# Issuing three chunks of block sums in the first FFN instead of beside the second mixer

## The chip, the cores and the metric

The kernel runs on one core of one Trainium2 chip. The time is the device time of one execution in microseconds, and the time of a kernel is the median of its runs. The profile is one further execution, recorded by the hardware profiler.

## What is computed

Two decoder layers over 512 tokens of 1024 features, in float32. Each layer adds a mixer (two kinds of attention side by side) and then a gated FFN to its input, with a normalisation before and after. The FFN matters here:

```python
def conv_ffn(h, w_up, conv_w, conv_b, w_down):
    u = causal_dwconv(h @ w_up, conv_w, conv_b)     # 1024 -> 2 x 2816, three taps along the tokens
    gate, up = jnp.split(u, 2, axis=-1)
    return (jax.nn.silu(gate) * up) @ w_down        # 2816 -> 1024
```

## The kernel before, in words

The order of the stages is `even` (first mixer), `ffn(0)`, `odd` (second mixer), `ffn(1)`. Every float32 operand of a large product is split into a high and a low part, and `mm3` (L343 to L347) makes three matmuls of each product: high by high, high by low, low by high.

**Weights.** The class `Weights` (L43) holds the list of all weight tiles in the order of their use. A tile of 128 by 1024 numbers is loaded from device memory by a DMA of the SyncE (SP) queue into one of three buffers `wraw` (`load`, L52 to L60). ScalarE (ACT) then makes the high part `wh` (L81) and VectorE (DVE) the low part `wl` (L82). There are five buffers for each part. A load can start when DVE has finished with the buffer's previous tile, and a split when TensorE (PE) has finished with a `wh`.

**The FFN's up stage.** `ffn` (L428) makes 22 pairs of output tiles, a gate and an up column block each, in the loop at L679 over `n`. Some of the pairs are made by a scheme of seven block products where the plain way has eight; that takes sums of blocks of the weights. `SEVEN` (L37) says which: in `ffn(0)` every second `n` from 4 to 18, in `ffn(1)` every `n` from 4 to 17.

- In `ffn(0)`, the sums of the weights' blocks are made on DVE from two raw tiles (`up_sums`, L175 to L202: L191, L192, L195 and L198 are the additions). Such a pair and the plain pair behind it need four loads together. `seven_sums` (L568) makes the products; two of its results, z2 (L587) and c22 (L591), are added on DVE and PE goes on adding to them.
- In `ffn(1)`, the sums come ready from device memory: `up_blocks` (L204) loads blocks of the tensors `ws` beside plain blocks (L57).

**The sums in device memory.** `make_sums` (L145 to L173) fills the `ws` tensors, for the 14 pairs of `ffn(1)`, in chunks of three pairs (`CHUNK`, five chunks). It uses only DMAs of the GpSimd (POOL) queue, from device memory to device memory, some of which add to what lies at the target. A chunk takes eight of them (`steps`, L164) in which each reads what the one before has written, at L161. The chunks of one call run four steps apart. Ahead of them, for each chunk, two DMAs of one number (L169) copy a `mark` into `ws`: the mark's only use is that the moves can't start before it is there. The call sets POOL's order by hand (`manual_schedule`, L166).

The first call (L1133) makes chunks 0 and 1 (`EARLY = 2`) during the first mixer. The second call (L1550) makes chunks 2, 3 and 4 in `odd`, behind its first projection. Its mark is a number that ACT copies into `lead` (L1549) from the last tile of that projection, `st`.

**What sets the order.** Where no order is written out by hand, the language's planner orders each engine's instructions at build time, by its own estimate of when each is ready. The up stage of `ffn(0)` and the first part of `odd` are ordered so, for PE, ACT and DVE; SP's queue always is. Each engine and each queue then runs its instructions in that fixed order, and one that waits holds up those behind it. Apart from DMA issues, POOL has only the small operations of the normalisations (L260 to L263).

Of the kernel before, what the change touches and what calls it, by code (L numbers as in the profile page):

```python
# [37 lines left out]
CHUNK = 3  # L38
PAIRS = len(SEVEN[1])
EARLY = 2  # L40
# [55 lines left out]
def trunk(tc, A, out):  # L96
    nc = tc.nc
    PE, ACT, DVE, POOL = nc.tensor, nc.scalar, nc.vector, nc.gpsimd

    with ExitStack() as top:  # L100
# [15 lines left out]
        def bank(tag, name, *shape):  # L116

            t = pp.tile([P, S], F32, tag=tag, name=name, bufs=BANKS[tag])
            if not shape:
                return t[:]  # L120
            n = math.prod(shape)
            names = "abc"[:len(shape)]
            return t[:, :n].rearrange(f"p ({' '.join(names)}) -> p {' '.join(names)}",
                                      **dict(zip(names, shape)))
# [4 lines left out]
        lead = cst.tile([P, 80], F32, tag="lead", name="lead")  # L129
# [15 lines left out]
        def make_sums(chunks, mark):  # L145

            wide = "(a q) c -> a (q c)"
            if not sums_of:
                sums_of[1] = [[dpool.tile([CHUNK * P, S], F32, tag=f"ws{j}{c}", name="ws")
                               for c in range(-(-PAIRS // CHUNK))] for j in range(4)]  # L150
            tiles = sums_of[1]

            def move(c, j, src, op=ALU.bypass):
                n = min(CHUNK, PAIRS - c * CHUNK) * P
                if src is None:
                    src = tiles[0][c][:n]
                elif src < 0:
                    src = tiles[1][c][:n]
                else:
                    src = A["ffn_up_q"][src, c * CHUNK * P:c * CHUNK * P + n]  # L160
                nc.gpsimd.dma_start(tiles[j][c][:n].rearrange(wide, q=4), src.rearrange(wide, q=4), accum_op=op,  # L161
                                    max_dma_last_dim=2048)

            steps = [(0, 3, ALU.bypass), (2, 2, ALU.bypass), (0, 2, ALU.add), (2, 0, ALU.add), (1, None, ALU.bypass),  # L164
                     (1, 0, ALU.add), (3, -1, ALU.bypass), (3, 1, ALU.add)]
            with tc.manual_schedule(engines={POOL.engine}):  # L166
                for c in chunks:
                    for j in (0, 2):
                        nc.gpsimd.dma_start(tiles[j][c][0:1, 0:1], mark)  # L169
                for n in range(len(steps) + 4 * len(chunks)):  # L170
                    for j, c in enumerate(chunks):
                        if 0 <= n - 4 * j < len(steps):
                            move(c, *steps[n - 4 * j])  # L173
# [169 lines left out]
        def mm3(o, lh, ll, rh, rl, first, last, more=False):  # L343

            PE.matmul(o, lh, rh, start=first, stop=False, skip_group_check=more)  # L345
            PE.matmul(o, lh, rl, start=False, stop=False, skip_group_check=more)  # L346
            PE.matmul(o, ll, rh, start=False, stop=last, skip_group_check=more)  # L347
# [80 lines left out]
        def ffn(layer, xnT, pending, final):  # L428
            with ExitStack() as es:
                fp = es.enter_context(tc.tile_pool(name=f"fp{layer}", bufs=1, reuse_waits="tile"))  # L430
                sp = es.enter_context(tc.tile_pool(name=f"fs{layer}", bufs=3, reuse_waits="tile"))
                cw = fp.tile([P, NF, 2, 4], F32, tag="cw", name="cw")
# [55 lines left out]
                def x_sums():  # L488

                    raw = [chp.tile([P, D], F32, tag="s", name="xsum") for _ in range(2)]  # L490
                    raw += [glob.tile([P, D], F32, tag=f"X{i}", name="xsum") for i in (3, 2)]
                    a, b, c, d = [r[:] for r in raw]

                    def whole_block(o, k0, t0):
                        h, l = x_block(k0, t0)
                        o = o.rearrange("p (a b) -> p a b", b=256)
                        DVE.tensor_tensor(o, h.bitcast(F32), l.bitcast(F32), ALU.add)

                    def sub(o, x, y):
                        DVE.tensor_tensor(o, x, y, ALU.subtract)  # L500

                    def minus(o, x, y):
                        DVE.scalar_tensor_tensor(o, x, -1.0, y, ALU.mult, ALU.subtract)

                    def parts(n, x):
                        h, l = sums[n]
                        return [lambda: ACT.copy(h[:], x), lambda: sub(l[:], x, h[:].bitcast(F32))]

                    return ([lambda: whole_block(a, 0, 0), lambda: whole_block(b, 0, 256), lambda: sub(a, a, b)]
                            + parts(0, a)  # L510
                            + [lambda: whole_block(c, 4, 256), lambda: sub(b, c, b)] + parts(2, b)
                            + [lambda: minus(c, c, a)] + parts(1, c)
                            + [lambda: whole_block(d, 4, 0), lambda: minus(d, d, c)] + parts(3, d))
# [96 lines left out]
                def begin_seven():  # L610

                    nonlocal begun
                    begun = [bank(t, "u") for t in "sa"]
                    c = begun[1][:, :256]
                    product(c, x_block(0, 0), True)
                    ACT.copy(begun[0][:, :256], c)
# [52 lines left out]
                def finish(left):  # L669

                    scale, conv, silu, rest = left
                    conv(0)
                    scale(1)
                    silu()
                    conv(1)
                    for step in rest:
                        step()

                for n, f in enumerate(PAIRED):  # L679
                    if n == 2:  # L680
                        for i in ORDER:
                            nc.sync.dma_start(spill[i * P:(i + 1) * P, :], X[i][:])
                    if n == (2 if final else 3):
                        for step in x_sums():
                            step()
                    if final and n == pairs[0]:
                        depth, W.depth = W.depth, 0
                        ready, stop = W.pos + 3, W.pos + (7 * PAIRS + 1) // 2 + 2
                        W.ahead(ready)
                        written = tc.manual_schedule(engines={PE.engine, DVE.engine, ACT.engine})  # L690
                        written.__enter__()
                        begin_seven()
                    if final and n in pairs:
                        left = seven(n, left)
                        if n == pairs[-1]:
                            for step in late:
                                step()
                            finish(left)
                            written.__exit__(None, None, None)
                            W.depth = depth  # L700
                        continue
                    u = u4[2 * n:2 * n + 2] if n < 2 else [bank(t, "u") for t in "sa"] if n in pairs else [None] * 2
                    y = sp.tile([P, 2, S], F32, tag="y", name="y")
                    if n in pairs:
                        seven_sums(u, y[:, 1, :256])
                    scale, conv, silu, rest = left = evict(n, y, u)
                    for z in range(2):
                        if u[z] is None:
                            u[z] = bank("as"[z], "u")
                            wh, wl = W.next()  # L710
                            for k in range(KD):
                                b = slice(k * P, (k + 1) * P)
                                mm3(u[z], wh[:, b], wl[:, b], xh[:, k], xl[:, k], k == 0, k == KD - 1)
                        if z == 0 or not final or n != pairs[0] - 1:
                            scale(z)
                        if not final or n != pairs[0] - 1:
                            conv(z)
                    if not final or n != pairs[0] - 1:
                        silu()
                        for step in rest:  # L720
                            step()
# [742 lines left out]
        def odd(xnT, pending, order):  # L1464
            xh, xl = xnT
            with ExitStack() as es:
# [59 lines left out]
                for i in ORDER:  # L1526
# [12 lines left out]
                    st = chp.tile([P, 512], F32, tag="s", name="vst")  # L1539
# [6 lines left out]
                nc.scalar.dma_start(tab12[:], A["dil_tab12"])  # L1546
                DVE.tensor_copy(tri[:], trif[:])

                ACT.copy(lead[0:1, 1:2], st[0:1, 0:1])  # L1549
                make_sums(range(EARLY, -(-PAIRS // CHUNK)), lead[0:1, 1:2])  # L1550


                for u in range(2):
                    proj_T(sq[u], 0.125, False, True)
# [319 lines left out]

        xnT = even()
        xnT = ffn(0, *xnT, False)
        xnT = odd(*xnT)
        ffn(1, *xnT, True)


# [101 lines left out]
```

## Time and profile before

| what | us |
|---|---|
| median of three runs | 1132.96 |
| lowest and highest run | 1132.69 and 1139.24 |
| span of the profiled execution | 1130.8 |
| time of that execution by the clock of the runs | not taken apart; the median lies 2.2 above its span |
| up stage of `ffn(0)` | about 236 to 446 |
| down stage of `ffn(0)` | about 446 to 580 |
| `odd` up to its output projection | about 580 to 762 |
| three chunks' moves on POOL, first to last issue | 613.5 to 747.4 |
| first load of a `ws` block for `ffn(1)` | 807.0 |

The span runs from the first to the last instruction of the profiled execution. A row of the view of groups or of the timeline gives an engine, a line, an operation, the tile written and the tiles read, the shapes, and times. A queue is written with a q behind its engine (SPq, POOLq). Idle time before an instruction stands in square brackets or behind a bar, with what ended it. In the view of stretches each engine has its busy time and its number of instructions.

### The profile page before, as it was taken

The page shows a single profiled execution, that of the slowest core. Times are in us where ns is not written, and L with a number is a line of the kernel's source. Part 1 is how long each engine was busy: PE and PEld are TensorE (multiplying, and loading weights), DVE is VectorE, ACT ScalarE, POOL GpSimd, SP SyncE. Part 2 cuts the span into 40 slices and gives each one's busy share as a digit, 9 for nine tenths or more (in the row PEclk, how much of TensorE's full clock was granted, in tenths as well). Part 3 has the DMA queues.
Part 4 walks back from the last instruction along what each step waited for, and adds up shares of the span by engine and source line. Part 5 has one row for each costly group of instructions (what it writes and reads, how often), then busy time and mean ns, then how long its engine had stood idle before and what let it go on. Part 6 is the DMA issues. An engine that isn't in the chain of part 4 may idle for free.

```text
span 1130.8 us, 17165 instructions
## 1 busy us (share of the span) xinstructions
PE 1118.5 (99%) x6432; PEld 951.1 (84%) x6432; DVE 898.1 (79%) x1526; ACT 624.9 (55%) x1060; POOL 96.0 (8%) x189
## 2 busy tenths in 40 slices
PE   9999999999999999999999999999999999999997
PEld 8876677898998998887888877888999999988886
DVE  6677476489998898898984476576889999989887
ACT  5565466446555555556653455575456666645662
POOL 2211012220000000000031111102000000000002
PEclk9999999999999999999999999999999999999999
DMA  8666731131422333354737878852335556524461
GB/s 296 197 180 137 215 109 57 57 134 57 130 94 79 128 94 121 99 168 151 226 128 227 206 186 202 217 122 85 110 112 182 179 182 196 177 89 148 144 205 75
DMA packets 61426, 166.82 MB, mean 148 GB/s; under 512 B 7841, under 2 KB 8993, under 8 KB 61217
## 3 DMA queue, kind: packets, MB, share of 16 engines
q1 hardware_dynamic: 47712, 132.65, 36.2%
q0 software_dynamic: 11712, 29.36, 11.8%
q10 hardware_dynamic: 1920, 3.74, 1.0%
q8 instruction: 50, 0.82, 0.3%
q14 instruction: 32, 0.25, 0.1%
HBM read 158.35 MB, written 35.68 MB: 172 GB/s over the span
## 4 chain that ended last, share of the span: by engine, by line
PE 88%; DVE 5%; DMA 3%; issue 2%; ACT 1%; POOL 0%; SPq 0%; POOLq 0%; DVEq 0%; ACTq 0%
PE u L345 12%; PE u L347 12%; PE u L346 12%; PE acc L345 4%; PE acc L346 4%; PE acc L347 4%; PE apt L345 3%; PE apt L346 3%; PE apt L347 2%; PE ao L345 2%; PE ao L347 2%; PE ao L346 2%; DVE wl L82 2%; PE sps L1170 2%; DMA wraw<-in_ffn_w_down 1%
## 5 line engine op out<-in xcount | busy, mean ns | idle before, releaser
L81 ACT CAST wh<-wraw 128x1024 fp32r<-128x1024 f32 (+1 forms) x235 | 240.7, 1033 | 158.0 <-PE u L346 51.6
L82 DVE TENSOR_TENSOR wl<-wraw,wh 128x1024 fp32r<-128x1024 f32 (+1 forms) x235 | 280.6, 1201 | 52.5 <-ACT wh L81 51.9
L345 PE MATMUL u<-xh,wh 128*128 128x256 f32 (+1 forms) x680 | 223.5, 329 | 0.0
L346 PE MATMUL u<-xl,wh 128*128 128x256 f32 (+1 forms) x680 | 223.1, 328 | 0.0
L347 PE MATMUL u<-xh,wl 128*128 128x256 f32 (+1 forms) x680 | 222.9, 328 | 0.0
L345 PEld LDWEIGHTS u<-xh,wh 128*128 128x128 f32 x680 | 129.2, 190 | 12.6 <-DVE u L587 1.3
L347 PEld LDWEIGHTS u<-xh,wl 128*128 128x128 f32 x680 | 129.1, 190 | 11.2 <-DVE wl L82 0.3
L346 PEld LDWEIGHTS u<-xl,wh 128*128 128x128 f32 x680 | 129.3, 190 | 11.0
L345 PE MATMUL acc<-wh,gh 128*128 128x512 f32 (+1 forms) x250 | 96.9, 388 | 0.8 <-DVE uu L758 0.8
L346 PE MATMUL acc<-wl,gh 128*128 128x512 f32 (+1 forms) x250 | 96.9, 388 | 0.0
L347 PE MATMUL acc<-wh,gl 128*128 128x512 f32 (+1 forms) x250 | 96.9, 387 | 0.0
L522 ACT ACTIVATE y<-u,cw 128x512 f32<-128x512 f32 x88 | 67.6, 777 | 36.9 <-PE u L347 33.4
L345 PE MATMUL u<-gh,wh 128*128 128x256 f32 x264 | 74.9, 284 | 0.1
L260 POOL TENSOR_TENSOR rv<-ms,epst 128x1 f32<-128x1 f32 x39 | 12.3, 314 | 736.3 <-ACT junk L312 351.2
L347 PE MATMUL u<-gh,wl 128*128 128x256 f32 x264 | 74.7, 283 | 0.0
L346 PE MATMUL u<-gl,wh 128*128 128x256 f32 x264 | 74.7, 283 | 0.0
L526 DVE SCALAR_TENSOR_TENSOR y<-u,cw,y 128x511 f32<-128x511 f32 x88 | 65.0, 743 | 3.5 <-ACT y L522 3.4
L528 DVE SCALAR_TENSOR_TENSOR y<-u,cw,y 128x510 f32<-128x510 f32 x88 | 65.3, 745 | 1.5
L345 PEld LDWEIGHTS acc<-wh,gh 128*128 128x128 f32 x250 | 46.9, 188 | 11.2 <-DVE uu L758 1.4
L347 PEld LDWEIGHTS acc<-wh,gl 128*128 128x128 f32 x250 | 47.0, 188 | 9.7
L346 PEld LDWEIGHTS acc<-wl,gh 128*128 128x128 f32 x250 | 47.0, 188 | 9.4
L345 PEld LDWEIGHTS u<-gh,wh 128*128 128x128 f32 x264 | 50.6, 192 | 1.3 <-ACT u L580 0.5
(371 smaller groups left out, 2420.8 us busy)
## 6 DMA issues: line engine op xcount, KB each, us to landing
wraw<-in_ffn_w_up SPq DMA_DIRECT2D x60, 512.0 KB, 3.7
wraw<-in_ffn_w_down SPq DMA_DIRECT2D x44, 512.0 KB, 3.7
ws<-in_ffn_up_q POOLq DMA_DIRECT2D x24, 768.0 KB, 7.6
wraw<-ws SPq DMA_DIRECT2D x56, 256.0 KB, 2.9
wraw<-in_ffn_up_q SPq DMA_DIRECT2D x42, 256.0 KB, 2.9
ws<-ws POOLq DMA_DIRECT2D x8, 768.0 KB, 6.4
wraw<-in_od_w_dqk SPq DMA_DIRECT2D x12, 512.0 KB, 4.4
wraw<-in_ffn_w_down SPq DMA_DIRECT2D x22, 256.0 KB, 2.8
```

The costliest lines, as they stand in the source:

```text
L81: self.nc.scalar.copy(h[:, :w], raw[:, :w])
L82: self.nc.vector.tensor_tensor(l[:, :w], raw[:, :w], h[:, :w].bitcast(F32), ALU.subtract)
L260: POOL.tensor_tensor(v[:, :n], ms, epst[:, :n], ALU.add)
L345: PE.matmul(o, lh, rh, start=first, stop=False, skip_group_check=more)
L346: PE.matmul(o, lh, rl, start=False, stop=False, skip_group_check=more)
L347: PE.matmul(o, ll, rh, start=False, stop=last, skip_group_check=more)
L522: ACT.activation(y[:, z], u[z], AF.Identity, bias=c[:, 3:4], scale=c[:, 2:3])
L526: DVE.scalar_tensor_tensor(y[:, z, 1:], u[z][:, :S - 1], c[:, 1:2], y[:, z, 1:], ALU.mult, ALU.add)
L528: DVE.scalar_tensor_tensor(y[:, z, 2:], u[z][:, :S - 2], c[:, 0:1], y[:, z, 2:], ALU.mult, ALU.add)
L1170: PE.matmul(s_ps[:, :w], mq[h][:, i * P:(i + 1) * P], mk[h][:, :w], start=True, stop=True)
```

## The change

The second call of `make_sums` moves from `odd` into `ffn`'s loop over `n`, at `n == 4` of `ffn(0)`, which is the first pair made of seven products. Its mark is now a number of `cw`, the tile of the convolution's coefficients, that is loaded once as `ffn(0)` begins (L433). The copy into `lead` in `odd` goes.

```diff
                     if n == (2 if final else 3):
                         for step in x_sums():
                             step()
+                    if n == 4 and not final:
+                        make_sums(range(EARLY, -(-PAIRS // CHUNK)), cw[0:1, 0, 0, 0:1])
                     if final and n == pairs[0]:
...
                 DVE.tensor_copy(tri[:], trif[:])
 
-                ACT.copy(lead[0:1, 1:2], st[0:1, 0:1])
-                make_sums(range(EARLY, -(-PAIRS // CHUNK)), lead[0:1, 1:2])
-
```

## The prediction

> **What bounds the kernel now.** I read the page's head first, then the chain of work that ended last.
>
> ```profile
> span 1130.8 us, 17165 instructions
> PE 1118.5 (99%) x6432; PEld 951.1 (84%) x6432; DVE 898.1 (79%) x1526; ACT 624.9 (55%) x1060; POOL 96.0 (8%) x189
> PE 88%; DVE 5%; DMA 3%; issue 2%; ACT 1%; POOL 0%; SPq 0%; POOLq 0%; DVEq 0%; ACTq 0%
> ```
>
> TensorE is busy for 1118.5 of 1130.8 us, so only 12.3 us of the span are without a matmul, and the chain lies on PE for 88%. Whatever moves can gain only where PE waits now, and lose only where it makes PE wait. So I compare the place that the three chunks leave with the place they go to, in the view of stretches (busy us of PE, PEld, DVE, ACT, POOL, each with its count; then PE's clock, DMA share, GB/s).
>
> ```profile
> 284.00:404.00 120.00, 119.93 (x758) 108.09 (x758) 109.89 (x159) 66.00 (x87) 0.00 (x0) 1.00 0.34 106
> 613.50:747.50 134.00, 133.31 (x768) 109.05 (x767) 80.12 (x196) 68.62 (x122) 17.93 (x24) 1.00 0.79 203
> 252.00:284.00 32.00, 32.00 (x184) 28.24 (x183) 30.67 (x40) 19.57 (x24) 0.00 (x0) 1.00 0.16 50
> ```
>
> The first row is the steady part of the first FFN's up stage: PE full, DVE at 92%, POOL empty, the DMA engines a third used. The second is the mixer while POOL issues the three chunks: PE idles 0.69 us, DVE is at 60%, the DMA engines are used to 0.79. The third is the start of the up stage, where DVE is at 96%. So the move takes DMA work out of a stretch where DVE has room and puts it into one where DVE has little.
>
> **Where the moved work would run.** POOL's timeline, and SP's row of the load that the new mark reads:
>
> ```profile
> 244.14 0.10 POOL L110 MEMSET spacer<- 128x1 f32 x1
> 568.56 0.73 POOL L260 TENSOR_TENSOR rv<-ms,epst 128x1 f32<-128x1 f32 x1 [324.32 <-ACT junk L312]
> 609.40 3.21 POOL L169 DMA_DIRECT2D ws<-lead  x6 [14.39 <-ACT lead L1549]
> 613.52 1.28 POOL L161 DMA_DIRECT2D ws<-in_ffn_up_q  x2 [0.90 <-DMA ws<-lead]
> 747.35 0.88 POOL L161 DMA_DIRECT2D ws<-in_ffn_up_q  x1 [3.53 <-DMA ws<-ws]
> 767.93 0.19 POOL L260 TENSOR_TENSOR rv<-ms,epst 128x1 f32<-128x1 f32 x1 [19.70 <-ACT junk L312]
> ...
> 243.95 0.38 SPq L433 DMA_DIRECT2D cw<-in_ffn_conv  x1
> cw<-in_ffn_conv SPq DMA_DIRECT2D x2, 88.0 KB, 3.8
> ```
>
> POOL does nothing between 244.14 and 568.56. The new mark needs only `cw`, issued at 243.95 and landed 3.8 us later, so about 247.8. The text puts the call at the fifth pair, but nothing on POOL waits for that pair, so I expect the six marks at about 248 and the first move about 4.1 us later (609.40 to 613.52 now), at 252. Should the planner put it at the fifth pair, at 284, the same sum holds with one pair later at either end.
>
> **The change part by part.**
>
> 1. Marks and moves on POOL: six issues of L169 in 3.21 us, then 24 of L161.
>
> ```profile
> L161 POOL DMA_DIRECT2D ws<-in_ffn_up_q x18: 575/916/1009, 613.5 to 747.4; - x18
> L161 POOL DMA_DIRECT2D ws<-ws x6: 591/616/927, 642.7 to 743.2; - x6
> L57 SPq DMA_DIRECT2D wraw<-ws x56: 319/323/1866, 807.0 to 959.1; - x56
> ```
>
> From first to last issue they take 133.9 us now, and PE sees nothing of POOL's own time. From 252 they would end at about 386. Behind them in POOL's queue stands the normalisation at 568.56, 182 us away: cost 0. Their readers, the loads of L57, begin at 807.0, which both places meet: 0. In the mixer POOL's next instruction is at 767.93, 20 us after the last move, so nothing waits for POOL there either: gain 0.
>
> 2. The copy at L1549 goes from ACT, and POOL's wait of 14.39 us with it. ACT is busy 68.62 of 134 us there: 0.
>
> 3. The mixer without the traffic. What does PE wait for there, and what do its loads cost?
>
> ```profile
> PEld run L1599 <- DVE z L1607: 1.6, 4, 0.6
> PEld z L1678 <- DVE st L1685: 0.7, 1, 0.7
> PEld z L1653 <- DVE wl L82: 0.7, 2, 0.4
> ACT wh L81 <- DMA wraw<-in_od_w_v: 0.7, 1, 0.7
> ACT wh L81 <- PE apt L346: 17.9, 7, 4.4
> ```
>
> These are us in total, times, longest. The first two are attention's own chain. Only 0.7 us wait for a weight, and ACT waits 17.9 us for PE to free a buffer, so the weights are ahead and a faster load buys little. Bounds: 0, and the three PE rows together, 3.0 us. The stretch's PE idle time, 0.69 us, is nearest; I take a gain of 0.5.
>
> 4. The first FFN's loads beside the traffic. The DMAs' bytes are the same in both places, so I take the traffic's share from the mixer (queue, packets, MB, share of 16 engines; first the up stage, then the mixer's two) and the landing times of `wraw` (min, median, max) in the same two stretches.
>
> ```profile
> q1 hardware_dynamic: 3456, 12.58, 33.1%
> DMA to landing us min/median/max: 3.3/3.7/4.9
> ...
> q0 software_dynamic: 6320, 16.25, 54.6%
> q1 hardware_dynamic: 4176, 10.86, 24.0%
> DMA to landing us min/median/max: 3.5/4.5/8.0
> ```
>
> 33.1% and 54.6% make 88%: the engines still suffice, and the moves should need little more than their 134 us. A load lands later by 4.5 - 3.7 = 0.8 us at the median and by 8.0 - 4.9 = 3.1 us at the worst. In the up stage loads come in close groups of three, like those that took 7 to 8 in the mixer, so I take the middle, 2.0 us. What covers it is the time from landing to use. One pair of tile pairs, in the timelines of SP, ACT, DVE and PE:
>
> ```profile
> 290.48 13.34 SPq L59 DMA_DIRECT2D wraw<-in_ffn_w_up  x2
> 305.77 2.12 SPq L185 DMA_DIRECT2D wraw<-in_ffn_w_up  x2
> 326.43 2.38 SPq L185 DMA_DIRECT2D wraw<-in_ffn_w_up  x2
> ...
> 308.70 1.05 ACT L81 CAST wh<-wraw 128x1024 fp32r<-128x1024 f32 x1 [0.99 <-PE u L346]
> 311.01 1.05 ACT L81 CAST wh<-wraw 128x1024 fp32r<-128x1024 f32 x1 [1.26 <-PE u L346]
> ...
> 312.45 1.22 DVE L82 TENSOR_TENSOR wl<-wraw,wh 128x1024 fp32r<-128x1024 f32 x1
> 314.73 0.68 DVE L191 TENSOR_TENSOR wraw<-wraw 128x512 f32<-128x512 f32 x1
> 315.33 0.42 DVE L591 TENSOR_TENSOR u<-u,y 128x256 f32<-128x256 f32 x1
> ...
> 316.11 0.28 PE L345 MATMUL u<-gh,wh 128*128 128x256 f32 x1
> ```
>
> The second load of the first row is issued at 290.48 + 13.34 - 0.33 = 303.49 (an issue takes 0.33), lands by the median at 307.2, and ACT uses it at 308.70, when PE frees a buffer: 1.5 us of cover. The next, at 305.77, lands at 309.5 and is used at 311.01: again 1.5. The third, at 307.56, lands at 311.3 for DVE's addition at 314.73: 3.4. With 2.0 us more the first two are 0.5 late, and the third is covered. ACT and DVE run in order, and DVE reaches L591 at 315.33 without a pause since 312.45. PE needs that sum at 316.11, 0.36 us after its end. So PE stalls between nothing (0.5 eaten by the 0.4 between the end of `wh` at 312.06 and DVE's start, and by the 0.36) and, with 3.1 late, about 0.8 to 2. I take 0.4 per pair of pairs, nearer the row than the worst. The pace is 20.6 us (326.43 - 305.77), so the moves from 252 to 386 lie beside the groups from 284 on, about six in all: 2.4 us, between 0 and 6 x 3.1 = 18.6.
>
> 5. The start, 252 to 284: DVE has 1.3 us to spare, and three loads lie there. I take 0.5, between 0 and 3.1.
>
> A rule bears on DVE beside POOL's issues. First the rows of the low part's subtraction (busy us, mean ns), in 300 to 440 and in 614 to 750:
>
> ```profile
> L82 DVE TENSOR_TENSOR wl<-wraw,wh 128x1024 fp32r<-128x1024 f32 x33 | 40.2, 1221 | 12.4 <-ACT wh L81 12.3
> L82 DVE TENSOR_TENSOR wl<-wraw,wh 128x1024 fp32r<-128x1024 f32 x17 | 20.8, 1223 | 15.2 <-ACT wh L81 15.2
> ```
>
> 1221 ns without the moves and 1223 with them: DVE isn't slowed. The Trainium skill, "SBUF — State Buffer", section "Terms", says of the shared port pair that VectorE and GpSimd lock a pair of SBUF ports for a whole instruction and the loser waits fully. By that rule issues could hold DVE; the trace does not agree as far as durations go. It is priced as a rival below, from rows.
>
> **Sum.** 2.4 + 0.5 - 0.5 = +2.4 us on the profiled span of 1130.8, so 1133.2. The median of the runs, 1132.96, lies 2.2 above that span; with it 1135.4, and I say 1135.
>
> **Rivals.**
>
> - *Late weights stall PE in each pair (slower).* For it: DVE has 10 us to spare in 120, and the sums L587 and L591 lie in the loop between PE and DVE. It decides when a load takes more than 3.7 + 1.5 + 0.8, about 6 us; the mixer had such (8.0). With 2.5 us lost in each of six, 15 us: 1148. Against it: ACT waits for PE, not for a DMA, in both quoted uses.
> - *The mixer gains what the FFN loses, or more (not slower).* Loads stay covered and part 3 gives 1 to 3 us: 1131. Against it: PE's waits in the mixer name DVE, and only 0.7 us a weight.
> - *POOL's issues hold DVE.* 24 issues of about 0.9 us are 21.6 us over 134, so 19 us in the 120 us stretch; DVE's 109.89 becomes 129, 9 more than the stretch: 1142. Against it: the two rows of L82.
> - *The planner orders the FFN or the mixer otherwise.* No row can price it. A real gain over 1% would have to take nearly all of the 12.3 us in which PE has no matmul.
>
> **How the numbers follow.** About 1%, 11.3 us, is what a measurement of this kernel tells from no change. The forecast (0 to +6 us) has 0.55, late weights 0.22, the mixer's gain 0.15, POOL against DVE 0.05, another order that is faster 0.03. Faster by over 1%: 0.03. Slower by over 1%: late weights, and two fifths of the DVE case: 0.24. Within 1%: 0.73. The range goes from 1130 (3.0 less than the median) to 1149, which takes in the likelier half of the late weights; the forecast's own is 1133 to 1139.
>
> **What would show it.** Right: POOL's `ws` issues from about 252 to 390; `wraw` landing at 5 to 6 us there; PE busy over 119 us in the 120 us from 284; the mixer's stretch unchanged within 1 us. Late weights: rows of ACT or DVE waiting for DMA `wraw`, and PE for L587 or L591, by more than 10 us in all. Wrong altogether: POOL still issuing at 568, or longer DVE instructions beside the moves.

## The result and the profile after

| kernel | median, us | ratio to before on the same chip (95% interval) |
|---|---|---|
| before, six runs beside the changed kernel | 1135.78 | 1 |
| changed, six runs | 1141.16 | 1.0051 [1.0027, 1.0076] |
| changed, once more, 12 runs against 35 of before (1133.45) | 1138.38 | 1.0042 [1.0025, 1.0058] |

The changed kernel is slower by about 0.45%, some 5 us. The time is inside the range and within 1%; the forecast was 1135, a ratio of 1.002. It lies above the forecast's own 1133 to 1139. Of the 6.2 us between 1135 and 1141.16, 2.8 are the kernel before itself, whose median is 1135.78 over six runs and was 1132.96 over the first three. First the page's head, with the chain's shares:

```profile
span 1139.2 us, 17167 instructions
PE 1121.1 (98%) x6432; PEld 950.6 (83%) x6432; DVE 898.4 (79%) x1526; ACT 624.4 (55%) x1059; POOL 96.5 (8%) x189
PE 74%; DVE 13%; DMA 7%; issue 3%; ACT 3%; POOL 0%; SPq 0%; DVEq 0%; POOLq 0%; ACTq 0%
```

DVE and DMA have gained 8 and 4 points of the chain at PE's cost, while DVE's work is the same to 0.3 us. So PE waits more often for the same work. The points are no measure of the loss: PE's 14 are 160 us of the span, the two executions lie 8.4 us apart, and in the second profile of the changed kernel (`c_after`, below) PE has 84%. The same three stretches:

```profile
252.00:284.00 32.00, 32.00 (x194) 28.71 (x193) 30.67 (x38) 17.89 (x21) 7.65 (x12) 1.00 0.60 151
284.00:404.00 120.00, 116.85 (x734) 104.55 (x733) 106.54 (x155) 64.08 (x85) 14.22 (x18) 1.00 0.80 214
613.50:747.50 134.00, 133.30 (x738) 107.95 (x736) 79.01 (x167) 66.97 (x103) 0.00 (x0) 1.00 0.31 94
```

The mixer lost its traffic (share 0.79 to 0.31) and PE gained nothing there: 133.30 against 133.31. The up stage took the traffic (0.34 to 0.80), and PE is without a matmul for 3.15 us where it had been for 0.07. POOL's timeline shows the moves where they were expected:

```profile
252.78 3.21 POOL L169 DMA_DIRECT2D ws<-cw  x6 [4.64 <-DMA cw<-in_ffn_conv]
...
398.36 0.88 POOL L161 DMA_DIRECT2D ws<-in_ffn_up_q  x1 [4.93 <-DMA ws<-ws]
576.37 0.64 POOL L260 TENSOR_TENSOR rv<-ms,epst 128x1 f32<-128x1 f32 x1 [177.13 <-ACT junk L312]
```

PE, ACT, DVE and SP run their instructions in the same order in both kernels (ACT but for the copy), so the two traces can be matched one to one: start of the same matmul after, less its start before.

| place | shift of PE, us | what it is |
|---|---|---|
| 232, end of the first mixer | +3.87 | scatter: the program is the same there (below) |
| 284, up stage before the first group | +3.90 | nothing lost at the start |
| 297, 317, 338 | +5.38, +6.63, +7.64 | three places, 3.74 us in all |
| 473 to 1075 | +7.64 to +7.80 | second mixer and second FFN: nothing |
| end | +8.44 | last down stage; `e_early_out` (below), whose three chunks stay in the mixer, loses 0.75 there |

Between the two profiled executions lie 8.4 us, but less than half of that is the change. The rest of the reading is in the three places. What PE waited for from 284 to 404, after (us in total, times, longest):

```profile
ACT wh L81 <- DMA wraw<-in_ffn_w_up: 9.0, 3, 3.6
...
PEld u L345 <- DVE u L591: 4.3, 3, 1.7
PE u L345 <- DVE u L591: 3.1, 3, 1.2
```

Before, ACT had no such row there, and L591 held only a weight load:

```profile
PEld u L345 <- DVE u L591: 0.3, 1, 0.3
```

And the landing of `wraw` in that stretch after (it was 3.3/3.7/4.9):

```profile
DMA to landing us min/median/max: 3.5/5.7/8.0
```

The second of the three places, in the timelines of SP, ACT, DVE and PE:

```profile
311.57 2.12 SPq L185 DMA_DIRECT2D wraw<-in_ffn_w_up  x2
...
318.20 1.05 ACT L81 CAST wh<-wraw 128x1024 fp32r<-128x1024 f32 x1 [3.06 <-DMA wraw<-in_ffn_w_up]
...
319.28 1.23 DVE L82 TENSOR_TENSOR wl<-wraw,wh 128x1024 fp32r<-128x1024 f32 x1 [1.35 <-ACT wh L81]
320.42 1.22 DVE L254 TENSOR_TENSOR gl<-y,gh 128x1024 fp32r<-128x1024 f32 x1
321.55 0.69 DVE L191 TENSOR_TENSOR wraw<-wraw 128x512 f32<-128x512 f32 x1
322.16 0.43 DVE L591 TENSOR_TENSOR u<-u,y 128x256 f32<-128x256 f32 x1
...
321.27 0.39 PE L346 MATMUL u<-xl,wh 128*128 128x512 f32 x1
322.64 0.38 PE L345 MATMUL u<-gh,wh 128*128 128x256 f32 x1 [0.98 <-DVE u L591]
```

Read it from the top. The load issued at 311.57 lands 6.55 us later; ACT has stood 3.06 us for it. DVE stands 1.35 us for ACT. Behind that low part, in DVE's fixed order, stand `gl`, an addition and the sum L591, and PE starts its next product 1.37 us after the last one, where it took 0.23 before. The low part that stood for the late load is three instructions ahead of the sum on DVE, which is why the row of PE's wait names a DVE sum and not a DMA.

### The profile page after: what moved, and what is told of

It is laid out like the page before. It is cut to its first block, busy times and chain, and to the rows that moved or that the text cites. A ratio compares the mean times of both kernels' runs of the same rounds, so it can differ in the third digit from the quotient of the medians.

```text
span 1139.2 us, 17167 instructions
## 1 busy us (share of the span) xinstructions
PE 1121.1 (98%) x6432; PEld 950.6 (83%) x6432; DVE 898.4 (79%) x1526; ACT 624.4 (55%) x1059; POOL 96.5 (8%) x189
## 3 DMA queue, kind: packets, MB, share of 16 engines
q10 hardware_dynamic: 1920, 3.74, 1.0%
## 4 chain that ended last, share of the span: by engine, by line
PE 74%; DVE 13%; DMA 7%; issue 3%; ACT 3%; POOL 0%; SPq 0%; DVEq 0%; POOLq 0%; ACTq 0%
PE u L345 10%; PE u L346 10%; PE u L347 10%; DVE wl L82 5%; DMA wraw<-in_ffn_w_down 3%; PE apt L345 3%; PE apt L346 3%; PE apt L347 2%; PE acc L345 2%; PE acc L347 2%; PE acc L346 2%; DMA wraw<-in_ffn_w_up 2%; PE ao L345 2%; PE ao L347 2%; PE ao L346 2%
## 5 line engine op out<-in xcount | busy, mean ns | idle before, releaser
L82 DVE TENSOR_TENSOR wl<-wraw,wh 128x1024 fp32r<-128x1024 f32 (+1 forms) x235 | 280.6, 1202 | 60.1 <-ACT wh L81 59.4
```

Of the source, the lines that this page charges most:

```text
L82: self.nc.vector.tensor_tensor(l[:, :w], raw[:, :w], h[:, :w].bitcast(F32), ALU.subtract)
```

## Experiments

In all of them PE's loss is read at the same points: the step of PE across each L591, less the 0.23 to 0.26 us that it takes before. The loss of the whole up stage is the growth of PE's shift from 284 to 446. Where PE waits at the sums alone, it is some 0.2 us larger than those steps, since the matmul behind each first one starts a little later too. A "group" is a pair with seven products and the plain pair behind it.

**Scatter and repetition.** `c_before` and `c_after` are the two kernels again.

> The kernel before, once more, unchanged. Theory (the cost sits in three places of the first FFN where PE waits for L591; what differs in the first mixer and in the last FFN's tail is scatter between executions): the ratio to the kernel before is 1.000 within 0.3%, and the profile shows the first mixer 0 to 5 us longer or shorter than in the first profile, with the same instructions, while 284 to 404 us (shifted by that) loses nothing. Rival (the first mixer's 3.9 us belong to the change): the first mixer's last matmul lies within 0.5 us of where it lay in the first profile.

> The changed kernel, once more, unchanged. Theory: 1.003 to 1.005 of the kernel before; the three waits of PE for L591 between 295 and 345 us come again at 3.0 to 4.5 us in all, and the first mixer's part of the delay differs from the 3.9 us of the first profile. Rival (the first mixer is made slower by the change): the first mixer is again 3.5 to 4.3 us behind the first profile of before.

`c_before`: 1133.57 us, 0.9995 [0.9981, 1.0009]. `c_after`: 1138.38, 1.0042 [1.0025, 1.0058]. The profile of `c_after` has +0.45 us at the end of the first mixer, where the first one had +3.87: that part was scatter. In the up stage it lost 2.8 us, 2.6 of them in the steps at L591, and nothing in the mixer. The stretch from 284 and its waits:

```profile
284.00:404.00 120.00, 117.78 (x747) 105.63 (x746) 107.63 (x156) 64.28 (x85) 14.08 (x18) 1.00 0.77 206
```

```profile
ACT wh L81 <- DMA wraw<-in_ffn_w_up: 5.1, 2, 3.6
PEld u L345 <- DVE u L591: 3.4, 3, 1.7
PE u L345 <- DVE u L591: 2.2, 2, 1.3
DVE wraw L191 <- DMA wraw<-in_ffn_w_up: 1.2, 1, 1.2
```

**The place that was left.** `e_nomoves` leaves the second call of `make_sums` out and adds nothing elsewhere.

```diff
+                if i // CHUNK >= EARLY:
+                    return A["ffn_up_q"][j - 4, i * P:(i + 1) * P]
...
-                make_sums(range(EARLY, -(-PAIRS // CHUNK)), lead[0:1, 1:2])
```

> Chunks 2 to 4 are not made at all: the second call of make_sums is left out, and the loads that read its sums in the second FFN read plain blocks of the weights of the same size instead, so the result is another one. Theory (the moves cost nothing in the second mixer and 3.8 us in the first FFN): the same as the kernel before, ratio 0.998 to 1.002, and no wait of PE for L591 over 0.5 us in the first FFN. Rival (the mixer pays for the moves too): 2 us or more faster than the kernel before, ratio under 0.998.

1133.55 us, 1.0007 [0.9997, 1.0018]. Without the moves anywhere the kernel is no faster than with them beside the mixer: they had been free there.

**POOL's issues or their bytes.** `e_tiny` has the changed kernel's issues, with 256 bytes of each row in place of 8 KB.

```diff
+                if c >= EARLY:
+                    o, src = o[:, :64], src[:, :64]
+                nc.gpsimd.dma_start(o, src, accum_op=op, max_dma_last_dim=2048)
```

> The changed kernel with the same six marks and 24 moves on POOL in the first FFN, but each moves 256 bytes of each of its rows instead of 8 KB (the readers read plain blocks of the weights instead, so the result is another one). Theory (the bytes make the loads land late): no cost, ratio 0.998 to 1.002, loads of wraw land at a median of 3.6 to 4.0 us between 284 and 404, no wait of PE for L591 over 0.5 us. Rival (POOL's issuing itself holds DVE or ACT): still 1.002 or more, with the three waits there.

1133.73 us, 1.0003 [0.9993, 1.0014]. The stretch from 284, and the landing of `wraw`:

```profile
284.00:404.00 120.00, 119.93 (x762) 108.18 (x761) 109.94 (x159) 66.77 (x88) 0.99 (x2) 1.00 0.32 106
```

```profile
DMA to landing us min/median/max: 3.4/3.8/5.0
```

The marks and the 24 issues ran from about 250 to 286, beside a DVE that is busy for 96% of that stretch, and cost nothing. They had ended before the groups that lose, so this run doesn't show POOL's issues beside those groups. What it shows is the loads beside the issues: the three issued from 256 to 261 landed after 4.2, 4.3 and 3.5 us. Before, each of the three took 3.6; in the changed kernel they took 5.5, 5.1 and 7.4. So most of the lateness belongs to the bytes.

**Half the bytes.** `e_half` is `e_tiny` with `[:, :1024]`, 4 KB of each row.

> The three chunks' moves in the first FFN with 4 KB in place of 8 KB of each row (half the bytes; the sums' readers read the plain blocks, so another result is computed). Theory (bytes of the traffic make loads land late, and the lateness has cover up to a point): the loads' median near 4.5 us, worst 6 to 7, loss 0 to 2 us, ratio 1.000 to 1.002. Rival (any sustained traffic there makes one load of three late, whatever its size): the loss of the full moves, 3 to 5 us, 1.003 to 1.0045.

1139.41 us, 1.0039 [1.0023, 1.0056]. Landing and waits from 284 to 404:

```profile
DMA to landing us min/median/max: 3.5/4.6/8.3
```

```profile
PEld u L350 <- DVE u L596: 3.7, 3, 2.4
PE u L350 <- DVE u L596: 2.6, 2, 1.9
```

(L596 is L591 here.) The rival is right. POOL's last move is issued at 332, not 398: half the bytes made the traffic shorter and not thinner (a DMA share of 0.80 from 284 to 332), and while it ran, loads landed nearly as late as in the changed kernel (from 284 to 340 a median of 5.9 us, where the changed kernel has 6.5). It ended behind the second group, and the whole loss, 2.1 and 0.8 us, lies in the first two. So the half that was spared had cost little: in the changed kernel only the third group's 1.0 us lies behind that point.

**The moves one chunk behind another.**

```diff
+                    if n == 4 and not final:
+                        for c in range(EARLY, -(-PAIRS // CHUNK)):
+                            make_sums([c], cw[0:1, 0, 0, 0:1])
```

> The changed kernel with the three chunks issued one behind another instead of four steps apart, so that fewer moves are in flight and the traffic is thinner and longer (252 to about 440 us). Theory (the loss follows how late the loads of the first three groups land): loads land at a median of 4.0 to 4.7 us, and PE's waits for L591 are 0.5 to 2.5 us in all; ratio 1.000 to 1.003. Rival (any traffic there costs the same, since one move at a time is as long in a load's way): 3 to 4.5 us as in the changed kernel, ratio 1.003 to 1.005.

1139.35 us, 1.0035 [1.0009, 1.0061]. The moves ran from 253 to 396 as before, with a DMA share of 0.78 in the stretch, and the profiled execution, the slowest of its 12, lost 6.7 us at four sums. Its up stage lost 8.5 in all, part of it in matmuls near 320 that ran longer, where the granted clock was 0.89. The rival is right: issuing them so thins nothing out.

**Six pairs later.** `e_late` makes the call at `n == 10`, with a mark that POOL can read only at 347.

```diff
+                    if n == 10 and not final:
+                        make_sums(range(EARLY, -(-PAIRS // CHUNK)), y[0:1, 0, 0:1])
```

> The changed kernel with the three chunks issued seven tile pairs of the loop later (at n == 10, with a number of the previous pair's y as mark), so that the moves start at about 347 us instead of 252 and end near 490. PE, DVE, ACT and SP have the same order of instructions. Theory (only the groups near 295, 316 and 337 us pay, where DVE's order puts splits and additions of just-loaded weights ahead of L591): no wait of PE for L591 over 0.5 us, ratio 0.999 to 1.002 if the down stage, which the moves then touch, has cover. Rival (every group beside the traffic pays by its late loads, and the first ones only by chance): 1.5 us or more lost between 347 and 490, ratio 1.0015 or more. If the loss comes in the down stage, PE waits there for acc or wl rows, which would be a third place.

1141.77 us, 1.0051 [1.0024, 1.0078]. The up stage lost only 0.7 us, although its loads from 347 to 440 landed as late as in the changed kernel:

```profile
DMA to landing us min/median/max: 3.4/5.5/8.6
```

But the moves ran until 495, into the down stage. The stretch from 420 to 560 and one of its waits, in this kernel:

```profile
420.00:560.00 140.00, 134.57 (x629) 110.20 (x628) 120.57 (x164) 74.66 (x99) 10.04 (x13) 1.00 0.70 193
```

```profile
DVE wraw L381 <- DMA wraw<-in_ffn_w_down: 9.9, 8, 2.3
```

and before:

```profile
420.00:560.00 140.00, 139.00 (x653) 115.87 (x653) 125.00 (x169) 78.97 (x106) 0.00 (x0) 1.00 0.47 147
```

```profile
DVE wraw L381 <- DMA wraw<-in_ffn_w_down: 3.8, 3, 1.4
```

The down stage lost 5.9 us, at six places from 481 to 541. At three of them, 494 to 512, PE waits for the low part of a weight (L82). But the last move landed at 503, and the places at both ends also lose in executions where no move runs beside them: 0.5 to 0.7 us at the first (`c_after`, `e_tiny`, `e_serial`), 1.9 at the last (`e_early_out`). So the later groups of the up stage have the cover for this traffic. That the stage behind them has less is likely, with the median as slow as the changed kernel's, but how much of the 5.9 us is the moves' is not shown.

**Is it the order on DVE?** In the three groups that lose, L591 stands behind the addition L191, which reads a third late load; in the later groups it stands ahead of it. `e_prio` gives L591 priority. That moves other instructions too, so `p_before` does it to the kernel before, as a control, and `e_prio_b` is `e_prio` again beside that control.

```diff
-                    DVE.tensor_tensor(c22, c21, p5, ALU.add)
+                    with tc.high_priority():
+                        DVE.tensor_tensor(c22, c21, p5, ALU.add)
```

> The changed kernel with its moves as they are, but the planner is told to give DVE's addition L591 a high priority, which puts it ahead of the split and the additions of the loads that come late in the first three groups (a few plain matmuls of PE move too). Theory (PE waits because L591 stands in DVE's queue behind a late load): most of the loss goes; waits of PE for L591 between 290 and 345 us fall from 3 to 4 us to under 1.2 us, while loads still land at a median over 4.5 us; ratio 0.999 to 1.002. Rival (the loss is the lateness of the weights for the matmuls themselves): the waits move to other rows of PE, 3 us or more are still lost, ratio 1.003 or more.

> The kernel before, with its second reduction sum L591 given priority over the additions of the loads (L191), the moves left in the mixer. It is the control for the same edit on the changed kernel. Theory: L591 behind L191 costs the kernel before nothing (its sums stood 0.4 us ahead of PE's need), and the other order moves a few instructions, so 1.000 to 1.003 of before. Rival: the priority itself costs the 3 to 4 us that the changed kernel with it lost (1.003 to 1.004), and then the moves cost that order nothing.

> The changed kernel with L591 given priority, once more, beside its control. Theory (the loss comes where L591 stands behind L191): within 1.5 us of the control, ratio to before as the control's. Rival (a late load holds DVE at whatever stands behind it, the order of the sum and the addition matters little): 2 to 4 us slower than the control.

`e_prio`: 1139.88, 1.0033 [1.0007, 1.0059]. `p_before`: 1134.81, 1.0008 [0.9991, 1.0025]. `e_prio_b`: 1140.16, 1.0046 [1.0026, 1.0066], 5.35 us over its control, which has the same order on PE and DVE. I had held the order to be the cause, and it is not. The control's first three groups leave their second load 4.7, 5.0 and 5.8 us from issue to use, much as the other order does, and beside the moves that load took 6.5, 6.5 and 7.8 in `e_prio_b`. DVE's timeline of `e_prio_b` in the second group (L592 is L591 here):

```profile
313.60 1.23 DVE L82 TENSOR_TENSOR wl<-wraw,wh 128x1024 fp32r<-128x1024 f32 x1 [2.24 <-ACT wh L81]
...
316.21 1.22 DVE L82 TENSOR_TENSOR wl<-wraw,wh 128x1024 fp32r<-128x1024 f32 x1
317.34 0.43 DVE L592 TENSOR_TENSOR u<-u,y 128x256 f32<-128x256 f32 x1
...
318.81 0.68 DVE L191 TENSOR_TENSOR wraw<-wraw 128x512 f32<-128x512 f32 x1
```

The sum is ahead of the addition now, but still behind two low parts, and the first of them stands 2.24 us for a load that took 6.9. PE's step there was 2.35 us.

**The other two chunks.** `e_early_out`, and `e_early_out_b` once more, move chunks 0 and 1 out of the first mixer to `n == 10` of the up stage, and leave the three in the second mixer.

```diff
+                    if n == 10 and not final:
+                        make_sums(range(EARLY), y[0:1, 0, 0:1])
...
-                        make_sums(range(EARLY), rk[0:1, 0:1])
```

> The kernel before with its first call moved: chunks 0 and 1 go from the first mixer to the first FFN at n == 10 (mark from the previous pair's y), chunks 2 to 4 stay in the second mixer. PE, DVE, ACT and SP have the same order. Theory (a load beside the moves costs where PE's cover is short; in the first mixer ACT waits 5.9 us for a load of w_dqk and the chain runs over DMAs there): the first mixer gets 1 to 4 us shorter and scatters less, the FFN loses nothing; ratio 0.996 to 0.999. Rival (the first mixer's waits for its loads have nothing to do with the moves): ratio 0.999 to 1.001.

> The kernel before with its other two chunks, those of the first mixer, made in the first FFN's up stage from the eleventh pair, and the three left in the second mixer; once more, for a closer interval. Theory (the first mixer gains the 1.6 us that the first profile showed, and the up stage from the eleventh pair has the order that loses nothing for two chunks): 0.997 to 0.999. Rival (the 1.6 us were scatter between executions, and a load is late there too): 1.000 to 1.003.

1134.22, 0.9987 [0.9964, 1.0009], and 1133.52, 0.9987 [0.9973, 1.0000]. Some 1.5 us faster, at the edge of what was measured. The stretch from 60 to 170 without the moves:

```profile
60.00:170.00 110.00, 109.91 (x539) 76.10 (x538) 76.89 (x256) 66.41 (x184) 6.42 (x15) 1.00 0.24 77
```

and before:

```profile
60.00:170.00 110.00, 108.69 (x533) 75.06 (x531) 75.66 (x251) 64.58 (x180) 15.31 (x26) 1.00 0.64 165
```

Matched against the first profile of before, PE at the end of the first mixer came 1.62 and 1.75 us earlier in these two. In the other 11 profiles, all with the moves in that mixer, it came 0.0 to 4.5 us later. Both are below all 12 with the moves. The up stage gave 0.2 and 0.9 of it back by 473 (0.4 of the 0.9 at 246, before these moves began), and the down stage 3.2 us in the first profile and 0.6 in the second, when the moves were over. In the first, DVE stood 3.1 us at L381 for one load of `w_down`, where it stood 1.0 before; why that load was late is not explained.

## Why the prediction was right, and where its steps were not

**1, marks and moves.** Right: nothing waits behind them on POOL. They ran from 252.8 to 398.4 (expected 248 to 386) in a trace that was 3.9 us late by then, and took 142 us from first to last issue, where it had been 134.

**2 and 3, the copy and the mixer.** I took a gain of 0.5; the mixer's gain was 0.0 in both profiles, and `e_nomoves` shows it by itself. The idle 0.69 us of PE that I leant on was still there without the traffic.

**4, the loads of the first FFN.** The mechanism is the one of the prediction, the rival's shape at the forecast's size: a load lands later, ACT and DVE stand for it, and PE waits at L591. The 2.0 us assumed were the measured rise of the median in the first profile (3.7 to 5.7; 4.7 in `c_after`). The term that failed is "0.4 per pair of pairs, about six in all". I read the cover of one group and multiplied. I also took the median, 3.7, for the landing of that group's second load, which took 4.1 in that trace, so that its 1.5 us of cover were 1.1; and (386 - 284) / 20.6 is five groups, not six. Before, the second late load of each group has this much time from issue to use, by ACT's and SP's timelines; the fifth group, say:

```profile
368.24 1.99 SPq L185 DMA_DIRECT2D wraw<-in_ffn_w_up  x2
...
374.57 1.05 ACT L81 CAST wh<-wraw 128x1024 fp32r<-128x1024 f32 x1
```

that is 6.3 us, where the second group, which the prediction quotes, has 311.01 - 305.77 = 5.2. The landing of that load, and PE's loss at the group's L591, in four profiles:

| group | issue to use before | changed | `c_after` | `e_serial` | `e_half` |
|---|---|---|---|---|---|
| 1 | 4.7 | 6.7, lost 1.4 | 6.7, lost 1.4 | 7.9, lost 2.6 | 7.4, lost 2.1 |
| 2 | 5.2 | 6.6, lost 1.1 | 5.0, lost 1.0 | 6.9, lost 2.1 | 6.2, lost 0.8 |
| 3 | 5.8 | 5.7, lost 1.0 | 4.0, lost 0.1 | 7.2, lost 1.5 | 4.5, lost 0 |
| 4 | 6.0 | 5.7, lost 0 | 6.1, lost 0 | 7.0, lost 0.6 | 4.6, lost 0 |
| 5 | 6.3 | 6.0, lost 0 | 4.5, lost 0 | 4.6, lost 0 | 3.9, lost 0 |

Where the landing is under the cover or barely above it, PE loses nothing; further above, it loses about the excess or some tenths less (6.7 - 4.7 = 2.0, lost 1.4). Four cells need another load of the group: the first one took 6.8 in the changed kernel's group 3 and 7.1 in group 2 of `e_serial`, and in `c_after` the third took 8.0 in group 2, where DVE stood 1.2 us for it at L191, and 7.1 in group 3. In these two cells the order on DVE does matter: behind L591, as in groups 4 and 5, the addition could not have held the sum. So the loss is not six times 0.4 but up to three times 1 to 1.4, and nothing behind. That 2.4 lies near the measured 2.8 and 3.7 is luck: it is too little for each group that lost and too much for the groups that lost nothing. The fifth group of the changed kernel shows how little was left:

```profile
382.21 1.05 ACT L81 CAST wh<-wraw 128x1024 fp32r<-128x1024 f32 x1
...
383.66 1.22 DVE L82 TENSOR_TENSOR wl<-wraw,wh 128x1024 fp32r<-128x1024 f32 x1
384.79 0.42 DVE L591 TENSOR_TENSOR u<-u,y 128x256 f32<-128x256 f32 x1
385.31 0.69 DVE L191 TENSOR_TENSOR wraw<-wraw 128x512 f32<-128x512 f32 x1
```

The load landed at 381.9, 0.3 us before ACT came to it from another cast, and DVE went through without a pause.

**5, the start.** I took 0.5; PE lost nothing there in either profile.

**The sum.** +2.4 was forecast: 2.4 + 0.5 - 0.5. The profiles show 2.8 and 3.7 in the up stage and nothing in the mixer that was left; the medians show 4.9 and 5.4. Single executions lost from 2.6 to 6.7 us at L591 with moves that start at 252, and the profiled execution of `c_after`, 1135.8, lies 2.6 below its kernel's median. So medians above these two profiles are no contradiction, but the last 2 us between them are not shown to lie at L591. Of the signs that I named, the times of the moves and the mixer came as said. PE busy for over 119 of 120 us did not: it was 116.85. For "late weights" I had named waits for `wraw` on ACT or DVE and PE's waits for the sums, over 10 us in all; they are 9.0 and 3.1. By its sign that rival came, and at 3.5 us of PE's time instead of 15. The range held it because it took in half of that rival.

**The rivals.** DVE's instructions are as long beside the moves as without them, in 300 to 440 after:

```profile
L82 DVE TENSOR_TENSOR wl<-wraw,wh 128x1024 fp32r<-128x1024 f32 x33 | 40.2, 1221 | 14.5 <-ACT wh L81 14.4
```

1221 ns, as before: POOL did not hold DVE, and `e_tiny` has the issues, up to 286, without the loss. The planner changed no order. As for why a load lands late: 512 KB took 3.7 us at the median where all DMAs together moved 106 GB/s, and 5.7 at 214. The two queues from 284 to 404 after (q0 carries the moves, q1 the loads; packets, MB, share of 16 engines):

```profile
q0 software_dynamic: 5272, 13.53, 49.9%
q1 hardware_dynamic: 3312, 12.06, 29.4%
```

Before, the 3456 packets of q1 had 33.1% of the 16 engines' 120 us, 0.18 us a packet; here it is 0.17. So the packets of the loads did not get slower, and a late load is one whose packets waited. The Trainium skill, "DMA: Bandwidth & Descriptors", section "Queues, rings and completion order", says that each DMA engine goes round its queues and drains a whole packet of one before it turns to the next. That fits `e_half`, where the bytes were halved and a load beside them was nearly as late; no view here shows which packet waited for which.

## What to carry to other kernels

A transfer off the critical path is paid for by the loads that land beside it: compare each load's time from issue to use with its landing time beside such traffic, group by group, since in a planned loop the cover differs from one round to the next (4.7 to 6.3 us here) and a total from one round is wrong for the rest. Background moves belong where loads are well ahead of their use, as in the second mixer here, where the moves cost nothing; halving them made the traffic shorter, not gentler. Where PE waits for a sum on DVE, look back in DVE's queue (three instructions here) for the one that stood for a load.

## What the runs showed of the hardware that was not expected

- Half the bytes per move left the lateness nearly as it was while the moves ran (from 284 to 340 a median landing of 5.9 us against 6.5, worst 8.3 against 8.0) and cut their length, from the first mark to the last issue, from 146 to 81 us.
- The same first mixer, with the same program, ended up to 4.5 us apart in 12 executions, all with moves from device memory to device memory beside its loads. In the two without them it ended within 0.13 us. This suggests that such traffic is a source of the scatter between runs; two executions don't prove it.
- Loads landed late, at a median of 5.7 us in place of 3.7, while a packet of theirs took 0.17 us, no longer than the 0.18 without the moves.
- 24 DMA issues and six marks on POOL from 250 to 286, beside a DVE busy for 96%, made no difference that 12 runs can show: 1.0003 [0.9993, 1.0014].
